# Two closing barriers replaced by one GpSimd wait, and fewer row-by-row instructions, in a streaming ReLU-and-sum kernel

## The chip, the cores and the metric

The kernel runs on one core of one Trainium2 chip. The metric is the device time of one execution in microseconds, as a median over several runs. All runs told here were in the fast state, at a granted clock of 1.00. The experiments ran in four sessions, each with the kernel before in the same rounds: e1 to e4 and e5 to e8 on the record's chip 0, e9 to e12 on chip 3, e13 to e16 on chip 10; the medians of the kernel before were 162.92, 163.09, 163.07 and 163.09 us. A difference of under 0.2 us between medians of different sessions means little. Engine names are those of the profile: DVE is VectorE, ACT is ScalarE, POOL is GpSimd, SP is SyncE, PE is TensorE.

## The reference

```python
x = np.random.randn(32, 512, 1024).astype(np.float32)   # 67.1 MB

def reference(x):
    return np.sum(np.maximum(x, 0), axis=-1).astype(np.float32)   # (32, 512)
```

It is 16,384 rows of 1,024 numbers. Each number is read once, so the work is a stream of 67 MB from memory.

## The kernel before

The rows are taken in seven blocks of 128 partitions x 16 rows and a tail of 8 + 4 + 2 + 1 rows and four column pieces of the last row. SP issues every load and store. A row can be worked on in two ways. In the two-step way ACT clamps several rows in place (`clamp`) and DVE adds them up (`total`), one instruction each. In the row-by-row way one engine clamps and adds a single row; the profile shows that each such operation is two instructions, the operation and a read of the accumulator (1044 and 187 ns on ACT, 1215 and 82 ns on DVE).

```python
TWO = [[16], [16], [16], [8, 8], [8, 8], [6, 5], []]   # rows of each two-step pair, by block
ACT = [0, 0, 0, 0, 0, 5, 8]                            # single rows on ScalarE
DVE = [0, 0, 0, 0, 0, 0, 8]                            # single rows on VectorE
TAIL = [8, 4, 2, 1]

    # ... in the entry function, after the body:
    nc.cur_bb = nc.bb_map[tc.start_bb_name + "_end"]
    body = nc.cur_bb.bb.instructions
    ends = list(body)                          # the framework's closing instructions
    body.clear()
    nc.sync.wait_ge(sems.stored, 16 * n_stores)
    body.extend(ends)                          # put back behind SyncE's wait
    # ...
    for n in TAIL:
        loaded = load(buf[:, c : c + n, :], rows(m, n), None if c else freed[NB - NBUF])
        for i in range(n):
            if i % 2 == 0:
                act_row(buf[:, c, :], m, loaded if i == 0 else None)
            else:
                dve_row(buf[:, c, :], res[:, m : m + 1], loaded if i == 1 else None)
            # ...
```

The framework's closing instructions are a barrier of all five engines, a GpSimd drain and a range clear of the program's semaphores 99 to 116, and a second barrier of all five engines; the trace records one update of each of these 18 semaphores between 160.30 and 160.38 us, when the clear runs. The program opens with a similar barrier, which ends at 0.78 us.

## Time and profile before

| | before |
|---|---|
| time, median of 3 runs | 163.16 us (163.13 to 163.45) |
| span of the program's own instructions | 160.70 us |
| 16-row loads land every | 19.4 us |
| last increment of the last load | 157.89 us |
| last increment of the last store | 159.90 us |

These are lines of the page of the kernel before: the span, the busy time of the engines, and the DMA queue with its packets, MB and share of 16 engines.

```profile
span 160.7 us, 162 instructions
...
DVE 117.0 (73%) x47; ACT 102.8 (64%) x52; POOL 0.2 (0%) x4
...
q1 hardware_dynamic: 2592, 67.18, 97.6%
```

The packets take 97.6% of the time of the 16 DMA engines, while DVE is busy 73% and ACT 64% of the span, and ACT's clamps alone sit idle for 47.2 us until loads land. The loads bound the kernel, and everything after the last load is a tail.

This is a stretch of the costliest groups, with shapes kept apart: line, engine, operation, tiles, count, then busy us and mean ns, then idle time before them.

```profile
L119 DVE TENSOR_REDUCE res<-io 128x8 f32<-128x8192 f32 x4 | 34.5, 8677 | 0.0
...
L126 ACT ACTIVATE io<-io 128x1024 f32<-128x1024 f32 x21 | 21.9, 1044 | 6.8 <-DMA io<-in_x_dram 6.8
L136 DVE TENSOR_SCALAR_CACHE_REDUCE io<-io 128x1024 f32<-128x1024 f32 x15 | 17.4, 1215 | 0.9 <-DMA io<-in_x_dram 0.8
L119 DVE TENSOR_REDUCE res<-io 128x6 f32<-128x6144 f32 x1 | 6.5, 6546 | 0.0
```

From 6 to 8 rows the sum grows by 2.13 us, which is 1.07 us a row. ACT's and DVE's single-row operations wait for loads (6.8 and 0.8 us), not the reverse.

The windows view of the kernel before, cut near the landings of block 7 (138.03), of the eight-row tail load (147.74) and of the last tail rows (155 to 156.4): busy us of DVE and ACT (with the number of instructions), the clock, DMA share and GB/s. In these windows block 6, block 7 and the first tail loads are worked on.

```profile
126.00:138.00 12.00, 11.98 (x3) 7.58 (x11) 0.00 (x0) 1.00 0.91 393
138.00:147.60 9.60, 9.21 (x16) 8.43 (x16) 0.00 (x0) 1.00 0.99 427
147.60:156.00 8.40, 7.86 (x13) 7.30 (x13) 0.00 (x0) 1.00 0.97 405
```

DVE has about 0.4 us to spare in the second window and 0.5 in the third; ACT has 1.2 and 1.1.

The timeline at the end of the kernel before (start us, us, what) and then the closing instructions, which all stand on L29 (duration ns min/median/max, first and last start us):

```profile
158.04 0.44 DVE L204 TENSOR_SCALAR_CACHE_REDUCE piece<-piece 128x271 f32<-128x271 f32 x1
158.40 0.08 DVE L204 DVE_READ_ACCUMULATOR piece<-piece 128x1 f32 x1
158.51 0.33 SPq L104 DMA_DIRECT2D out_dram<-res  x1
```

```profile
L29 POOLq EVENT_SEMAPHORE  x4: 17/17/17, 160.0 to 160.6; - x4
L29 POOLq DRAIN  x3: 34/41/82, 0.7 to 160.4; - x3
L29 SPq DRAIN  x3: 7/7/7, 159.9 to 160.2; - x3
...
L29 PEldq EVENT_SEMAPHORE  x2: 51/51/51, 160.1 to 160.7; - x2
L29 POOLq EVENT_SEMAPHORE_RANGE_CLEAR  x1: 136/136/136, 160.3 to 160.3; - x1
```

SP sees the store at 159.92, the first barrier runs to about 160.2, the clear ends at 160.41, the second barrier ends the program at 160.70.

The measured time is longer than the span. The trace's semaphore records go on past the last instruction of the program and show what follows. These are times in us from the program's first instruction; semaphore 2, which no instruction of the program uses, is incremented in chains of nine, which I read as a barrier, five engines up and four down. I call all that follows the program the runtime's; the records name no owner. Of the 249 semaphores from 7 to 255, 247 have one record each between 161.36 and 162.02 us, which I read as resets. The first closing chain takes 0.52 us, the resets 0.66, the second chain 0.43.

```
kernel before, increments of semaphore 2
opening   -0.37  -0.34  -0.30  -0.26  -0.23  -0.12  -0.08  -0.05  -0.00
closing 1 160.94 160.97 161.18 161.22 161.24 161.34 161.38 161.41 161.46
          (semaphores 7 to 255 are reset between 161.36 and 162.02)
closing 2 162.25 162.36 162.40 162.44 162.46 162.56 162.60 162.63 162.68
instruction packets of 8192 bytes: seven before -8 us, one at 162.81, 0.57 us long
```

The last line of that block comes from the trace's DMA records.

### The profile page before, as it was taken

How to read it: one execution, taken by the hardware profiler on the slowest of the kernel's cores; microseconds unless marked ns; L12 is line 12 of the kernel's file. 1: busy time of each engine (PE TensorE's matmuls, PEld its weight loads, DVE VectorE, ACT ScalarE, POOL GpSimd, SP SyncE). 2: the span in 40 equal slices, each digit the busy share in tenths (PEclk: the TensorE clock that was granted, in tenths of full speed). 3: DMA queues.
4: the chain of work that ended last, by engine and by line, in shares of the span. 5: the costliest groups of instructions: out<-in, count | busy, mean ns of one | idle time of the engine just before them, and what ended most of it. 6: DMA issues, size and time to landing. Idle time of an engine off the chain costs nothing.

```text
span 160.7 us, 162 instructions
## 1 busy us (share of the span) xinstructions
DVE 117.0 (73%) x47; ACT 102.8 (64%) x52; POOL 0.2 (0%) x4
## 2 busy tenths in 40 slices
DVE  0000000009999499994999999999999999998984
ACT  3000059990799709995099932999249992696882
POOL 0000000000000000000000000000000000000000
DMA  7996996996996996996996996996996997998992
GB/s 261 522 522 261 522 522 261 522 522 261 522 522 261 522 522 261 522 506 277 522 489 294 522 489 294 522 489 294 522 489 294 522 440 343 392 481 371 424 389 47
DMA packets 2592, 67.18 MB, mean 418 GB/s; under 512 B 672, under 2 KB 1184, under 8 KB 1312
## 3 DMA queue, kind: packets, MB, share of 16 engines
q1 hardware_dynamic: 2592, 67.18, 97.6%
HBM read 67.11 MB, written 0.07 MB: 418 GB/s over the span
## 4 chain that ended last, share of the span: by engine, by line
DMA 43%; DVE 33%; ACT 17%; another core or an unknown queue 3%; SPq 1%; issue 0%; DVEq 0%
DVE res L119 32%; DMA io<-in_x_dram 25%; DMA piece<-in_x_dram 18%; ACT io L111 17%; SPq L93 1%; DVE piece L136 1%; DVE piece L204 0%; DVEq L29 0%
## 5 line engine op out<-in xcount | busy, mean ns | idle before, releaser
L119 DVE TENSOR_REDUCE res<-io 128x8 f32<-128x8192 f32 (+3 forms) x9 | 97.9, 10933 | 40.1 <-ACT io L111 40.1
L111 ACT ACTIVATE io<-io 128x8192 f32<-128x8192 f32 (+3 forms) x9 | 79.2, 8826 | 47.2 <-DMA io<-in_x_dram 47.2
L126 ACT ACTIVATE io<-io 128x1024 f32<-128x1024 f32 x21 | 21.9, 1044 | 6.8 <-DMA io<-in_x_dram 6.8
L136 DVE TENSOR_SCALAR_CACHE_REDUCE io<-io 128x1024 f32<-128x1024 f32 x15 | 17.4, 1215 | 0.9 <-DMA io<-in_x_dram 0.8
L126 ACT ACTIVATION_READ_ACCUMULATOR io<-io 128x1 f32 x21 | 3.9, 187 | 0.0
L111 ACT ACT_TABLE_LOAD x1 | 1.3, 1283 | 0.8 <-PEq L249 0.8
L136 DVE TENSOR_SCALAR_CACHE_REDUCE piece<-piece 128x244 f32<-128x244 f32 (+2 forms) x3 | 1.2, 416 | 0.4 <-DMA piece<-in_x_dram 0.4
L136 DVE DVE_READ_ACCUMULATOR io<-io 128x1 f32 x15 | 1.2, 82 | 0.0
L204 DVE TENSOR_SCALAR_CACHE_REDUCE piece<-piece 128x271 f32<-128x271 f32 x1 | 0.4, 436 | 0.0
L136 DVE DVE_READ_ACCUMULATOR piece<-piece 128x1 f32 x3 | 0.2, 82 | 0.0
L249 POOL MEMSET const-bfloat16-1.0<- 128x1 bf16 x1 | 0.1, 102 | 0.0
L249 POOL MEMSET const-uint8-127<- 128x1 uint8 x1 | 0.1, 101 | 0.0
L249 POOL MEMSET const-float32-0.0<- 128x1 f32 x1 | 0.1, 99 | 0.2 <-issue 0.2
L249 POOL MEMSET const-float32-1.0<- 128x1 f32 x1 | 0.1, 98 | 0.0
L204 DVE DVE_READ_ACCUMULATOR piece<-piece 128x1 f32 x1 | 0.1, 84 | 0.0
## 6 DMA issues: line engine op xcount, KB each, us to landing
io<-in_x_dram SPq DMA_DIRECT2D x1, 4096.0 KB, 21.6
io<-in_x_dram SPq DMA_DIRECT2D x1, 2048.0 KB, 26.1
io<-in_x_dram SPq DMA_DIRECT2D x1, 1024.0 KB, 28.1
io<-in_x_dram SPq DMA_DIRECT2D x1, 512.0 KB, 28.9
piece<-in_x_dram SPq DMA_DIRECT2D x1, 134.0 KB, 28.4
piece<-in_x_dram SPq DMA_DIRECT2D x1, 130.0 KB, 28.6
piece<-in_x_dram SPq DMA_DIRECT2D x1, 126.0 KB, 28.7
piece<-in_x_dram SPq DMA_DIRECT2D x1, 122.0 KB, 28.8
```

The source lines that it names most:

```text
L93: dma = nc.sync.dma_start(out=dst, in_=src)
L111: i = nc.scalar.activation(out=ap, in_=ap, func=RELU)
L119: nc.vector.tensor_reduce(out=res[:, m : m + n], in_=ap, axis=mybir.AxisListType.X, op=ADD).wait_op(sems.act, n_act, "sem-ge").then_inc(se ...
L126: i = nc.scalar.activation(out=ap, in_=ap, func=RELU, accum_out=res[:, m : m + 1])
L136: i = nc.vector.tensor_scalar(out=ap, in0=ap, scalar1=0.0, scalar2=None, op0=MAX, op1=ADD, accum_out=accum_out,)
L204: nc.vector.tensor_scalar(out=last[:, :], in0=last[:, :], scalar1=0.0, scalar2=None, op0=MAX, op1=ADD, accum_out=res[:, NT - 1 : NT],).wai ...
L249: nc = _bacc.Bacc("TRN2", target_bir_lowering=False, num_devices=1)
```

## The change

The intent: the closing barriers only order the clear of the semaphores against engines that still use them, and once every store has landed no engine does. So GpSimd waits for the stores itself and clears; the other engines end when their work ends. In the sixth and seventh block and the tail, rows move so that fewer instructions are needed: block 6 from sums of 6 + 5 rows and 5 single rows to sums of 7 + 7 and 2 single rows; block 7 from 8 and 8 single rows on ACT and DVE to 9 and 7; the eight-row tail load from 4 and 4 to 5 and 3.

```diff
-TWO = [[16], [16], [16], [8, 8], [8, 8], [6, 5], []]
-ACT = [0, 0, 0, 0, 0, 5, 8]
-DVE = [0, 0, 0, 0, 0, 0, 8]
+TWO = [[16], [16], [16], [8, 8], [8, 8], [7, 7], []]
+ACT = [0, 0, 0, 0, 0, 2, 9]
+DVE = [0, 0, 0, 0, 0, 0, 7]
@@
-    ends = list(body)
+    clear = semaphore_clear(body)      # GpSimd's drain and range clear alone
     body.clear()
-    nc.sync.wait_ge(sems.stored, 16 * n_stores)
-    body.extend(ends)
+    nc.gpsimd.wait_ge(sems.stored, 16 * n_stores)
+    body.extend(clear)
@@
-            if i % 2 == 0:
+            if i % 2 == 0 or (n == 8 and i == 7):
                 act_row(buf[:, c, :], m, loaded if i == 0 else None)
```

The helper `semaphore_clear` picks the two GpSimd instructions.

More of the change, by code (lines that the diff above doesn't have):

```diff
@@ L215, in relu_sum, with semaphore_clear @@
     return n_store
+def semaphore_clear(instructions):
+    pool = [i for i in instructions if i.engine == mybir.EngineType.Pool]
+    at = next(
+        n for n, i in enumerate(pool) if getattr(i, "is_reset_sema", False)
+    )
+    return pool[at : at + 2]
 def issue_ahead_of_the_barrier(tc: tile.TileContext, n_loads: int):
```

## The prediction

> **What bounds the kernel now.** The input stream. The page shows DMA engines 97.6% busy over the 160.7 us span; 16-row blocks land every 19.4 us (semaphore records). DVE is busy 73%, ACT 64%. Loads are queued well ahead: the tail loads are issued at 126.16 us while block 7 lands at 138.03. So the last input piece lands at 157.89 whatever DVE and ACT do, if they keep up. The timeline then ends so: four small DVE sums (the last ends at 158.48), 1 KB store issued at 158.51, its last increment at 159.90, then the closing: SP sees the store (159.92), barrier, GpSimd range clear (136 ns, ends 160.41), second barrier, end at 160.70.
>
> The measured time (163.14 in the profiled run) is longer than the span. The semaphore records show why: a chain of nine increments of semaphore 2 runs from 160.94 to 161.46, some 250 semaphores are reset (to 162.02), a second chain ends at 162.68. With 0.37 us of an opening chain that makes 163.05. [...] this trace shows 0.52, 0.66 and 0.43. In the first chain the third increment comes 205 ns after the second; hops in the opening chain take 23 to 44, but for its turn: the third engine is late. [...] it is GpSimd (my inference), which ended at 160.61 and arrived 0.56 us later.
>
> **What the change does.**
> 1. Ending. Two all-engine barriers go. GpSimd waits for the stores itself, drains (34 to 82 ns), clears (136 ns). Estimate: wait over at 159.92, clear ends at about 160.15, against GpSimd's last instruction at 160.61 before: 0.46 us earlier, all on the critical path, since GpSimd is already the late one at the runtime's barrier. The span shortens by 0.5 to 0.6 us (its last instruction before was PE's, 0.09 us after GpSimd's); the runtime's part stays.
> 2. Rows. Block 6: DVE sums 14 rows rather than 11, at 1.07 us a row (8677 and 6546 ns for 8 and 6 rows); ACT loses three row instructions of 1.04. Estimate: DVE ends the block at 141.2 rather than 138.0, block 7 with seven rows (1.14 us apart) at 149.2 rather than 147.3, its three rows of the eight-row tail load at 152.5, before the next load lands at 152.65. ACT, with five rows there, starts the next 0.3 us late and catches up by 155.15. Both are level before the last pieces; gain 0. It only uses up slack.
>
> Sum: 163.16 - 0.46 = **162.7 us**, range 162.4 to 163.1. Chances: faster by over 2% 0.01, within 2% 0.98, slower by over 2% 0.01.
>
> **What would show it.** Span near 160.15; the clear ending about 0.25 us after the last store increment; semaphore 2's first increments long before the end, GpSimd's about 0.56 us after the clear, the chain done by about 161.0; last piece landing near 157.9, last DVE sum ending near 158.5; no DVE idle before block 7.
>
> **What would make it wrong.** GpSimd waking slowly from a long wait, or its 0.56 us growing; runs differing by 0.3 us (163.13 to 163.45 before) hiding the gain; DVE running late into the pieces: 0.4 us of slack is left at 156.4.

163.16 less the 0.46 of the ending and 0 of the rows is 162.7. The 0.52, 0.66 and 0.43 us are the first closing chain, the resets and the second chain of the trace of before. The 0.56 us runs from GpSimd's last instruction (160.61) to the third increment (161.18); that the third engine is GpSimd was an inference.

## The result, and the profile after

| | before | after |
|---|---|---|
| median | 163.14 us (162.99 to 163.45, 4 runs) | 161.98 us (161.94 to 162.01, 4 runs) |
| span | 160.70 | 160.06 |
| last increment of the last load | 157.89 | 157.80 |
| last increment of the last store | 159.90 | 159.79 |
| last increment of semaphore 2 | 162.68 | 162.06 |
| time of the profiled run | 163.14 | 161.95 |

The ratio is 0.9926, with a 95% interval of 0.9909 to 0.9943. A ratio is the mean time of one kernel's fast runs over that of the other's of the same rounds, so it is not quite the ratio of the medians quoted. The gain is 1.16 us where 0.46 was predicted, and 161.98 lies below the range of 162.4 to 163.1.

The same lines of the page after:

```profile
span 160.1 us, 133 instructions
...
DVE 117.7 (74%) x43; ACT 104.2 (65%) x50; POOL 0.2 (0%) x4
...
q1 hardware_dynamic: 2592, 67.18, 98.0%
```

```profile
L120 DVE TENSOR_REDUCE res<-io 128x8 f32<-128x8192 f32 x4 | 34.5, 8676 | 0.0
L127 ACT ACTIVATE io<-io 128x1024 f32<-128x1024 f32 x20 | 20.9, 1043 | 5.4 <-DMA io<-in_x_dram 5.3
L120 DVE TENSOR_REDUCE res<-io 128x7 f32<-128x7168 f32 x2 | 15.1, 7608 | 0.0
L137 DVE TENSOR_SCALAR_CACHE_REDUCE io<-io 128x1024 f32<-128x1024 f32 x13 | 15.0, 1214 | 0.2
```

The instructions cost what they cost before, and the seven-row sum is where interpolation put it (7608 ns). DVE and ACT are together busier by 2.1 us, not less. So no time was won by doing less work. The windows say where the work went:

```profile
126.00:138.00 12.00, 12.00 (x3) 6.97 (x6) 0.00 (x0) 1.00 0.91 393
138.00:147.60 9.60, 9.60 (x12) 9.41 (x18) 0.00 (x0) 1.00 0.99 428
147.60:156.00 8.40, 8.19 (x15) 8.34 (x15) 0.00 (x0) 1.00 0.98 407
```

In the second window DVE has no idle time left and ACT 0.2 us; in the third 0.2 and 0.1. The slack is used up and nothing else happens. The end of the timeline of the kernel after is as before, a tenth of a microsecond earlier, because the loads landed that much earlier in this trace; a later trace of this same kernel (e7) has the last load at 157.98, so that is no effect of the change.

```profile
157.92 0.43 DVE L205 TENSOR_SCALAR_CACHE_REDUCE piece<-piece 128x271 f32<-128x271 f32 x1
158.28 0.08 DVE L205 DVE_READ_ACCUMULATOR piece<-piece 128x1 f32 x1
158.39 0.33 SPq L105 DMA_DIRECT2D out_dram<-res  x1
```

The closing lines of the kernel after (all of L29):

```profile
L29 POOLq DRAIN  x1: 88/88/88, 159.8 to 159.8; - x1
L29 POOLq EVENT_SEMAPHORE_RANGE_CLEAR  x1: 136/136/136, 159.9 to 159.9; - x1
```

Two instructions are left of the two barriers and the clear. The records past the end:

```
kernel after, increments of semaphore 2
closing 1   1.00 157.60 160.59 160.63 160.66 160.75 160.79 160.83 160.87
closing 2 161.70 161.74 161.78 161.82 161.84 161.94 161.98 162.01 162.06
instruction packets of 8192 bytes: five before -8 us, none later
```

Two engines now reach the runtime's barrier early (1.00 and 157.60; the last instructions of TensorE and ScalarE end 0.23 and 0.11 us earlier), and the third holds it up, 0.53 us after GpSimd's clear. That this third engine is GpSimd was an inference before; now GpSimd is the only engine that still has anything to do (the last instruction of any other, SyncE's issue of the last store, ends at 158.73). The profiled runs differ by 163.14 - 161.95 = 1.19 us. The records split it into three: the last store landed 0.11 earlier; from the last store to the last increment of semaphore 2 it takes 2.27 instead of 2.78, which is 0.51; and the measured time now stands 0.11 us below the time of that last increment where it stood 0.46 above it, which is 0.57. (A value below zero shows that the measured time cannot be counted from the program's first instruction to that increment; where it starts and ends, no run says.) I call this last difference, measured time minus time of the last increment of semaphore 2, the surplus. Of the 0.51, 0.47 lies before the end of the first closing chain and is the predicted term; the other 0.04 lies in the reset and the second chain. The 0.57 was not in the prediction at all.

One part of the prediction that looked right was luck. It added the 0.37 us of the opening chain to the last increment and got 163.05, close to the measured 163.14. The same sum for the kernel after is 162.06 + 0.37 = 162.43, against a measured 161.95. So the measured time is not that sum, and its agreement before hid a term. (A slip besides: the prediction gives the hops of the opening chain as 23 to 44 ns, but the last one takes 47.)

### The profile page after: what moved, and what is told of

Its sections match the earlier page's. It is cut to its first block, busy times and chain, and to the rows that moved or that the text cites. A ratio compares the mean times of both kernels' runs of the same rounds, so it can differ in the third digit from the quotient of the medians.

```text
span 160.1 us, 133 instructions
## 1 busy us (share of the span) xinstructions
DVE 117.7 (74%) x43; ACT 104.2 (65%) x50; POOL 0.2 (0%) x4
## 4 chain that ended last, share of the span: by engine, by line
DMA 43%; DVE 33%; ACT 17%; another core or an unknown queue 3%; SPq 1%; issue 0%
DVE res L120 32%; DMA io<-in_x_dram 25%; DMA piece<-in_x_dram 18%; ACT io L112 17%; SPq L94 1%; DVE piece L137 1%; DVE piece L205 0%
## 5 line engine op out<-in xcount | busy, mean ns | idle before, releaser
L120 DVE TENSOR_REDUCE res<-io 128x8 f32<-128x8192 f32 (+2 forms) x9 | 101.1, 11287 | 40.0 <-ACT io L112 40.0
L112 ACT ACTIVATE io<-io 128x8192 f32<-128x8192 f32 (+2 forms) x9 | 81.7, 9110 | 47.1 <-DMA io<-in_x_dram 47.1
L127 ACT ACTIVATE io<-io 128x1024 f32<-128x1024 f32 x20 | 20.9, 1043 | 5.4 <-DMA io<-in_x_dram 5.3
L137 DVE TENSOR_SCALAR_CACHE_REDUCE io<-io 128x1024 f32<-128x1024 f32 x13 | 15.0, 1214 | 0.2
```

Of the source, the lines that this page charges most:

```text
L112: i = nc.scalar.activation(out=ap, in_=ap, func=RELU)
L120: nc.vector.tensor_reduce(out=res[:, m : m + n], in_=ap, axis=mybir.AxisListType.X, op=ADD).wait_op(sems.act, n_act, "sem-ge").then_inc(se ...
L127: i = nc.scalar.activation(out=ap, in_=ap, func=RELU, accum_out=res[:, m : m + 1])
L137: i = nc.vector.tensor_scalar(out=ap, in0=ap, scalar1=0.0, scalar2=None, op0=MAX, op1=ADD, accum_out=accum_out,)
```

## The experiments

The question is what moved the surplus from +0.46 to -0.11. My theory: the length of an engine's instruction stream decides it. The kernel before has 58 instructions on ScalarE and 54 on VectorE as the trace counts them, the kernel after 52 and 46, and the trace of before has an 8 KB instruction packet after the runtime's last barrier that the trace of after does not have. The rival: the runtime's ending is quicker simply because four engines arrive early.

To lengthen a stream without delaying anything I add waits that are already satisfied, where the engine idles anyway (in the kernel after, ScalarE's clamps wait 47.1 us in all for loads and VectorE's sums 40.0 for ScalarE). The compiler packs two such waits into one instruction, which I did not know: the pads came out half as long as their expectations say (six waits made 3 instructions in e3, eight made 4 in e4).

### e1: the new ending alone

```diff
 # the kernel after, with
-TWO = [..., [7, 7], []]; ACT = [..., 2, 9]; DVE = [..., 0, 7]
+TWO = [..., [6, 5], []]; ACT = [..., 5, 8]; DVE = [..., 0, 8]
-            if i % 2 == 0 or (n == 8 and i == 7):
+            if i % 2 == 0:
```

> The new ending with the old rows. Theory F (part of the gain beyond the ending is one 8 KB instruction fetch that in the kernel before starts at 162.81 us, after the runtime's last barrier, takes 0.57 us and is gone after the change because an engine's instruction stream got shorter): if the fetch belongs to GpSimd, SP or PE, whose streams shorten only by the ending, it is gone and the time is about 162.0; if it belongs to ScalarE or VectorE it may stay (their ending also lost 4 instructions each, the rows 2 and 4 more), and the time is then about 162.6. Rival R (the tail of the runtime is shorter only because four engines arrive early): about 162.0 whatever the trace says of fetches. Last chain of semaphore 2 ends near 162.1 in all cases.

Measured 162.22 us against 162.92 of the kernel before in the same rounds (ratio 0.9951). Last increment of semaphore 2 at 162.12, as expected. No late packet, and a surplus of 0.115, between the two values. The rival, which wanted 162.0, misses 0.2 us; the theory in its simple form misses it too.

### e2: the new rows alone

```diff
 # the kernel before, with the new TWO, ACT, DVE and
-            if i % 2 == 0:
+            if i % 2 == 0 or (n == 8 and i == 7):
```

> The old ending with the new rows. Theory F: if the row instructions alone take the late fetch away, about 162.5 and no instruction packet after time 0; if not, 163.1 with one near 162.8. Rival R: 163.1, since the ending is the old one. First barrier chain of semaphore 2 with GpSimd late as before.

Measured 162.59 against 162.92 (ratio 0.9974). No late packet; surplus -0.08. The ending is the old one, so the rival cannot explain the gain: it falls as a sole cause. In the second closing chain of semaphore 2 the eighth of the nine increments comes 0.13 us late.

### e3 and e4: the kernel after, with a longer ScalarE, and with a longer VectorE

```diff
 # e3, after the first clamp            # e4, before the first sum
+for _ in range(6):                     +for _ in range(8):
+    nc.scalar.wait_ge(sems.loads[0], 16)  +    nc.vector.wait_ge(sems.act, 1)
```

> The changed kernel with 6 waits on ScalarE that are already satisfied, put where ScalarE idles (after its first clamp), so that ScalarE's stream is as long as before. Theory F, if the fetch is ScalarE's: it comes back, about 162.5. If it is another engine's, or by rival R: 161.98.

> The changed kernel with 8 satisfied waits on VectorE before its second sum, so that VectorE's stream is as long as before. Theory F, if the fetch is VectorE's: it comes back, about 162.5. Otherwise, or by rival R: 161.98.

e3: 162.24, surplus 0.22, with ScalarE at 55 instructions (not 58). Its profiled run, 162.58, was held up by a late last load (158.10), which the surplus does not contain. e4: 162.04, surplus -0.11, with VectorE at 50 (not 54). Three instructions that cost nothing where they stand add 0.26 us to the median on ScalarE (against the 161.98 of the result); four on VectorE add nothing up to 50.

### e5, e7: the two kernels again

> The kernel before, unchanged, for a second trace of it. If the late 8 KB instruction packet (162.81 us in the first trace) and the time after the last increment of semaphore 2 (0.46 us more than that increment's time) are a fixed part of this kernel, both are seen again: a packet after 162 us and a surplus over 0.3 us. If the packet was a chance of one execution, it is absent and the surplus is smaller. Time equal to the kernel before by construction; the difference shows the noise.

> The changed kernel, unchanged, on this chip and in these rounds, for a second trace and a fair neighbour: 161.98 again, 5 instruction packets of 8 KB, none late, last increment of semaphore 2 later than the measured time by about 0.1 us.

e5: 163.14, against 163.09 of the same kernel in the same rounds; late packet at 162.89, surplus 0.42. e7: 161.98, surplus -0.11, no late packet. Packet and surplus are there in both traces of the kernel before. The number of early packets is not a property of a kernel: six here for e7, five in the first trace of the same kernel, so I draw nothing from it.

### e6: both pads

```diff
+for _ in range(6): nc.scalar.wait_ge(sems.loads[0], 16)
+for _ in range(8): nc.vector.wait_ge(sems.act, 1)
```

> The changed kernel with both pads: 6 satisfied waits on ScalarE and 8 on VectorE, so that both streams are as long as before while the ending stays new. If the two engines' lengths together make the late fetch: about 162.5 to 162.6 and 7 or 8 instruction packets of 8 KB instead of 5. If lengths of ScalarE alone matter, as the first four runs hint (162.24 with its pad, 162.04 with VectorE's): about 162.24. If length plays no part: 161.98.

Median 162.48 (162.24 to 162.57), and in the profiled run 162.24 with a surplus of 0.225, no late packet. Streams of 55 and 50. The surplus is that of e3, and so is the profiled run; the median is higher by a quarter of a microsecond. The record shows that this does not lie in the ending: the spans of the three slower runs are 160.2 to 160.4 us against 160.0, and time minus span is 2.17 to 2.24 us in all four.

### e8: SyncE waits, and nobody clears

```diff
-    clear = semaphore_clear(body)
     body.clear()
-    nc.gpsimd.wait_ge(sems.stored, 16 * n_stores)
-    body.extend(clear)
+    nc.sync.wait_ge(sems.stored, 16 * n_stores)
```

> A further step: SP waits for the stores instead of GpSimd, and nobody clears the program's semaphores (the records show that the runtime resets 7 to 255 at its end anyway). Against the changed kernel this takes away GpSimd's drain and clear (0.25 us) and its 0.53 us from clear to the runtime's barrier; SP[...] then needs about 0.25 us as PE did. Theory: about 0.45 us less than the changed kernel, 161.5. If a later part of the runtime's ending is bound by something else, less. Correct in repeated executions only if the runtime's reset does cover the semaphores.

Measured 161.36 against 161.98 of e7 and 163.09 of the kernel before in the same rounds (ratio to before 0.9893), correct in every run. It beats both kernels. Its one closing instruction:

```profile
L41 SPq EVENT_SEMAPHORE  x1: 17/17/17, 160.0 to 160.0; - x1
```

SyncE's increment of semaphore 2 comes 0.11 us after it, not the 0.25 that I had estimated from TensorE (0.24 in the trace of before). From the last store to the last increment of semaphore 2 it takes 1.49 us (2.27 in the kernel after). The surplus stays at -0.12.

### e11: GpSimd waits, and nobody clears

```diff
     body.clear()
     nc.gpsimd.wait_ge(sems.stored, 16 * n_stores)
-    body.extend(clear)
```

> The changed kernel without the drain and range clear: GpSimd only waits for the stores. Splits the 0.6 us by which SP waiting without a clear beat the changed kernel. Drain, gap and clear take 0.25 us in the changed kernel's trace, so about 161.7 if GpSimd's 0.53 us from its last instruction to the runtime's barrier stays; 161.4 if that interval is caused by the drain and clear and goes with them.

Measured 161.76 (161.63 to 161.93). GpSimd's wait ends at 159.84, its increment comes at 160.38: the interval of 0.54 us stays without drain and clear. So of the 0.62 us that e8 wins, about 0.22 is drain and clear (161.98 to 161.76, from different rounds), and the rest is mostly GpSimd's slow way to the barrier. From the last store to the last increment of semaphore 2 the traces give 2.27 (after), 2.05 (e11) and 1.49 us (e8), so 0.22 and 0.56; the medians show less of the second part because the last store landed later in e8's trace (159.96) than in e11's (159.80).

### e9 and e10: old ending, new rows, one stream at a time as long as before

```diff
 # e9                                    # e10
+for _ in range(4):                      +for _ in range(8):
+    nc.scalar.wait_ge(sems.loads[0], 16)   +    nc.vector.wait_ge(sems.act, 1)
```

> Old ending, new rows, plus 4 satisfied waits on ScalarE, which the compiler packs two to an instruction: ScalarE has 58 instructions as before, VectorE 50. Theory A (ScalarE's length alone sets how long the program's end takes): back to the time before, 163.0 to 163.1, with a late 8 KB instruction packet near 162.8 and ScalarE late in the runtime's second barrier. If the late packet is VectorE's: no late packet, about 162.6.

> Old ending, new rows, plus 8 satisfied waits on VectorE in 4 instructions: VectorE has 54 as before, ScalarE 56. Theory A: 162.6 as without the pad, no late packet. If the late packet is VectorE's: 163.0 to 163.1 and a late packet near 162.8.

e9 (58 and 50): 162.59 (three runs within 162.56 to 162.61, one at 163.12), surplus -0.12, no late packet; the second increment of the second chain is 0.08 us late, as in the kernel before. e10 (56 and 54): 162.72, surplus -0.01, no late packet, the eighth increment 0.12 late. Neither brings the 163.07 of the same rounds back. Theory A, ScalarE alone, falls, and so does VectorE alone.

### e12: a still shorter ScalarE

```diff
 # block 6's two single rows in one instruction (their sums are wrong on purpose)
+            act_row(buf[:, c : c + 2, :], m + c, act_waits)
+            nc.vector.memset(res[:, m + c + 1 : m + c + 2], 0.0)
```

> The changed kernel with ScalarE shortened to 50 instructions by adding two rows in one instruction (the result of these two rows is wrong on purpose; one tiny VectorE memset fills the other column). Surplus of the measured time over the last increment of semaphore 2 so far: -0.11 us at 52 instructions, 0.115 at 54, 0.22 at 55, a line of 0.11 us an instruction. If 52 already lies on a floor: -0.11 and 161.98. If the line goes on: -0.33 and about 161.75.

At 50 instructions: 162.10, surplus -0.11. So 52 is on the floor and shortening further buys nothing. The line of 0.11 us an instruction was a line through three points and no more.

### e13, e14, e15: the new ending with both streams as long as before, and each alone

```diff
 # e13: VectorE only; e15: ScalarE only; e14: both
+for _ in range(12): nc.scalar.wait_ge(sems.loads[0], 16)
+for _ in range(16): nc.vector.wait_ge(sems.act, 1)
```

> The changed kernel with 16 satisfied waits on VectorE (8 instructions): VectorE 54 as before, ScalarE 52. If VectorE's length makes the late packet by itself: packet near 162.2, surplus about 0.4, time about 162.5. If both lengths are needed: surplus -0.11, 161.98.

> The changed kernel with 12 satisfied waits on ScalarE and 16 on VectorE: both streams as long as before (58 and 54), new ending. If both together make the late packet, whatever the ending: packet near 162.2, surplus about 0.45, time about 162.5, and ScalarE 0.08 us late in the second chain. If the old ending is needed too: no packet.

> The changed kernel with ScalarE alone at 58 (VectorE 46). By the old-ending run at 58: ScalarE 0.08 us late in the second chain, surplus -0.11, about 162.1. By the line of 0.11 us an instruction from 52 to 55: surplus 0.55, about 162.6.

e14: 162.56, surplus 0.38, and an 8 KB instruction packet at 162.32. The late packet is back, with the new ending and the new rows. e13: 162.29, surplus 0.16, no packet in the trace. e15: 162.19, surplus -0.11, the second increment of the second chain 0.05 late. The closing lines of e14 show that its ending is the changed one:

```profile
L29 POOLq DRAIN  x1: 87/87/87, 159.9 to 159.9; - x1
L29 POOLq EVENT_SEMAPHORE_RANGE_CLEAR  x1: 136/136/136, 160.0 to 160.0; - x1
```

### e16: the kernel before, with a shorter VectorE

```diff
 # block 7: four of VectorE's rows in one instruction (wrong on purpose)
+            dve_row(buf[:, c : c + 4, :], res[:, m + c : m + c + 1], dve_waits)
+            nc.vector.memset(res[:, m + c + 1 : m + c + 4], 0.0)
```

> The kernel before with VectorE alone shorter (four of its rows added in one instruction, result wrong on purpose, and one memset; about 49 instead of 54 instructions), ScalarE 58, old ending, nothing else. If VectorE's length causes the late packet: it is gone, surplus -0.11, about 162.55. If ScalarE's 58 or the old rows cause it: still there, 163.1.

162.52 against 163.09 (ratio 0.9967), late packet gone, surplus -0.12. Old ending, old ScalarE; only VectorE's stream is five instructions shorter. This is the expected first case.

### All of them

ACT and DVE are instruction counts of the trace; hitch is by how much one increment of the second chain is late against the 0.034 us of a usual hop; times are medians.

| run | ending | ACT | DVE | hitch | surplus | late packet | us |
|---|---|---|---|---|---|---|---|
| before, e5 | old | 58 | 54 | 0.08, 0.09 | 0.46, 0.42 | yes, yes | 163.14, 163.14 |
| e9 | old | 58 | 50 | 0.08 | -0.12 | no | 162.59 |
| e16 | old | 58 | 49 | 0.08 | -0.12 | no | 162.52 |
| e10 | old | 56 | 54 | 0.12 | -0.01 | no | 162.72 |
| e2 | old | 56 | 50 | 0.13 | -0.08 | no | 162.59 |
| e14 | new | 58 | 54 | 0.05 | 0.38 | yes | 162.56 |
| e15 | new | 58 | 46 | 0.05 | -0.11 | no | 162.19 |
| e13 | new | 52 | 54 | none | 0.16 | no | 162.29 |
| e6 | new | 55 | 50 | none | 0.23 | no | 162.48 |
| e3 | new | 55 | 46 | none | 0.22 | no | 162.24 |
| e1 | new | 54 | 50 | none | 0.12 | no | 162.22 |
| e4 | new | 52 | 50 | none | -0.11 | no | 162.04 |
| after, e7 | new | 52 | 46 | none | -0.11, -0.11 | no, no | 161.98, 161.98 |
| e12 | new | 50 | 47 | none | -0.11 | no | 162.10 |

These are second closing chains that the readings rest on, with ScalarE's and VectorE's counts and the measured time of the same run (us):

```
               1st    2nd    3rd    4th    5th    6th    7th    8th    9th   measured
before 58 54  162.25 162.36 162.40 162.44 162.46 162.56 162.60 162.63 162.68  163.14
e16    58 49  162.22 162.33 162.37 162.41 162.44 162.53 162.57 162.61 162.65  162.53
e2     56 50  162.16 162.19 162.23 162.27 162.30 162.40 162.43 162.60 162.64  162.56
e14    58 54  161.79 161.87 161.91 161.95 161.97 162.07 162.11 162.14 162.19  162.57
after  52 46  161.70 161.74 161.78 161.82 161.84 161.94 161.98 162.01 162.06  161.95
```

A surplus comes from one traced run each, but the record has the time and the span (to 0.1 us) of every run. Time minus span is 2.17 to 2.71 us in all 32 later runs of the kernel before, and 1.81 to 1.92 in the eight of e9 and e16, which have the same ending. With the new ending it is 1.84 to 1.93 in after, e4, e7 and e12, 2.07 to 2.25 in e1, e3, e6 and e13, and 2.39 to 2.55 in e14. One run does not fit: e15 has 1.92 to 1.97 in three runs and 2.49 in the fourth, which has no trace.

The column of surplus reads as follows. VectorE at 50 or less adds nothing; at 54 it adds 0.27 us beside a ScalarE of 52 (e13 against e4), 0.49 beside one of 58 (e14 against e15), 0.54 to 0.58 with the old ending (before and e5 against e9), but only 0.07 beside one of 56 (e10 against e2). ScalarE adds 0.23 at 54 and 0.33 at 55; at 56 and 58 it adds little there and makes a hitch of 0.05 to 0.13 us in the barrier instead. The hitch has a place: at 58 it is always the second increment that is late, at 56 the eighth. In the first closing chain the second increment comes 0.11 us after ScalarE's last instruction in after, e8, e11 and e14, so it is ScalarE's; if the four increments down run in reverse order, the eighth is ScalarE's too.

## Why the prediction was wrong

**The stream bounds the kernel: right.** Last load 157.89 and 157.80, whatever the rows did. **The rows use up slack and gain nothing by their work: right.** DVE ended block 6 at 141.08 (predicted 141.2) and entered the four-row tail load at 152.55, the moment after it landed; ACT started there 0.33 us late (predicted 0.3) and had caught up at 155.04.

**The ending: right.** From the last store to the end of the runtime's first chain it took 1.56 us before and 1.09 after, a gain of 0.47 where 0.46 was predicted; GpSimd's increment came 0.53 us after its clear (predicted 0.56), the first increments came long before the end, and the span ended at 160.06 (predicted near 160.15). With streams as long as before, the new ending gives 162.56 against 163.09 (e14): 0.53 us.

**The step that failed** is "the runtime's part stays", and with it "gain 0. It only uses up slack" for the rows. I costed an instruction by the time it takes on its engine and took the time after the program as a constant. The runs show that this time depends on how many instructions the program has on VectorE and ScalarE: 0.57 us between before and after. e14 to the kernel after is 162.56 to 161.98, by length alone, with the same ending and the same rows. Within one session, e14 against e15 (162.56 against 162.19) differs by eight instructions of satisfied waits on VectorE and nothing else. The most direct proof is e16: five VectorE instructions fewer in the kernel before, and 0.57 us are gone (it changes what VectorE computes, too; the pads of e14 do not). In the change both halves shorten the streams: the ending takes four instructions off each of the two engines, the rows another two off ScalarE and four off VectorE. I had the packet of 162.81 us in the trace of before and did not ask about it, although I had followed the same records up to 162.68.

**What stays open** is the mechanism: no run shows how the length of a stream moves the end. What one would have to explain is this. The surplus comes at 54 and 55 instructions on ScalarE and turns into a hitch at 56 and 58 (0.05 to 0.13 us), first at the eighth increment and then at the second. The three late packets took 0.57, 0.53 and 0.47 us beside surpluses of 0.46, 0.42 and 0.38: each ends 0.22 to 0.24 us after the measured time. But the packet after the end is in the traces of before, e5 and e14 alone; e1, e3, e6 and e13 have a surplus of 0.12 to 0.23 (0.23 to 0.34 above the floor) and no such packet. Whether their packets were not recorded or do not exist, no run says. That VectorE's 54 cost so little beside 56 on ScalarE (e10) is in good part bookkeeping, since the surplus counts from the ninth increment, which the hitch at the eighth delays. From the sixth increment, which lies before the hitch, to the measured time it is 0.23 us in e10, 0.28 in e13, 0.17 in e2 and 0.01 in e4. Why it is 0.50 to 0.58 us with ScalarE at 58 (before, e5, e14) is open, and so is e15's one long run.

## What to carry to other kernels

Where a kernel ends at a floor that its data set, look past its last instruction: who arrives last at the runtime's barrier, and what the records show after it. A wait for the stores belongs on an engine that reaches that barrier fast, here SyncE rather than GpSimd (0.11 us from its last instruction to its increment, against 0.53, or 0.54 with nothing but a wait before it; TensorE took 0.24 and ScalarE 0.11), and the program's own clear is not needed where the runtime resets the same semaphores, as it did here (e8, 161.36 us, 1.1% below the kernel before; its trace records the reset of 17 of the 18 semaphores; e8 and e11, without a clear, were correct in all their runs). When instructions are removed and the time falls by more than their work, or by work that was off the critical path, pad one engine's stream with satisfied waits and see whether length alone brings the time back.
